# Smaller first loads on two queues, fewer warm-up products and a split that reads the PSUM bank twice, in a two-layer decoder step on one core

## The chip, the core and the metric

The kernel runs on one core of a Trainium2 chip. TensorE (PE) multiplies, VectorE (DVE) and ScalarE (ACT) do elementwise work, GpSimd (POOL) and SyncE (SP) mostly issue DMAs. ACT also issues DMAs from its own queue. The metric is the device time of one execution in microseconds. The time before is the median of three runs.

## The reference, cut to what matters

One inference step of a decoder with two layers, for a prompt of 512 tokens and for 8 samples of one token each, 520 columns in all. Model width 1024, feed-forward width 2816.

```python
for l in range(2):
    x = x + 0.5 * swiglu(rms(x, g[l, 0]), w_gate[l, 0], w_up[l, 0], w_down[l, 0])
    # layer 0: causal pooling over windows 2, 4, 8, 16; layer 1: window attention with sinks
    x = x + mixer(rms(x, g[l, 1]))
    x = x + 0.5 * swiglu(rms(x, g[l, 2]), w_gate[l, 1], w_up[l, 1], w_down[l, 1])
y = rms(x, final_g)
```

`swiglu(h) = (silu(h @ w_gate) * (h @ w_up)) @ w_down`. All inputs are fp32. The study is about the very first part, in which x is loaded and transposed and the first 128 columns of `w_gate[0, 0]` and `w_up[0, 0]` are multiplied with it.

## The kernel before, in words

**Products in three terms.** Each fp32 operand is split into a high part (fp32r) and a rest: ACT writes the high part as a rounded copy (`xh`, `wh`), DVE subtracts it from the source (`xl`, `wl`). A product is the sum of `wh*xh`, `wh*xl` and `wl*xh`. The 520 columns are taken in two halves of 260, so one 128x128 piece of weights costs six PE instructions (function `mm`, L413 to L424).

**Layout.** x stands transposed: eight tiles `x[0..7]` of 128 channels by 520 tokens. Weights arrive in chunks of 1 MB (`raw`, three buffers), are cut into pieces of up to four 128x128 blocks, and each piece is split by ACT (L194, `wh`) and DVE (L195, `wl`). The class `Weights` holds the plan: `chunk` and `piece` enter it, `begin` issues the first loads of a chunk, `load` the rest, `get` returns the next split piece, `prefetch` splits some pieces ahead.

**The start (L662 to L739).** x comes from memory as tokens by channels. Loads `xt` (L667) bring 256 tokens by 256 channels (256 KB) each, so that two loads together hold two tiles; `load_x(nc.sync, ...)` puts them on SP's queue, `load_x(nc.scalar, ...)` on ACT's. `grow` (L671) holds the norm gains, `xs` (L674) the samples. PE multiplies ones with ones (L698, twelve calls, 24 records in the trace, as each fp32 product shows as two) and so is busy until the loads are there. Then it transposes the gains (L699), which ACT copies to `gT` (L700).

`x_tile(k)` (L702 to L718) makes tile k: four transposes of the prompt and one of the samples into a PSUM tile (L707, L709), `xh` by ACT with the gain as scale (L712), a copy of the plain tile to SBUF (by ACT for odd k, L714, by DVE for even k, L716), and `xl` by DVE from that SBUF copy (L717).

**The first products.** Tiles 0 and 1 are made first. Then for each k the six products with the gate piece are issued, tile k+2 is made, and the six products with the up piece follow. So PE does five transposes between the two groups, and the transposes of a tile stand two steps ahead of its products.

**What sets the order.** Instructions passed through `later` keep the program's order; a scheduler orders the others. Each engine runs its own in order, so one that waits holds up all behind it. PSUM has four double banks. In the first phase they are used so: one for the gate accumulator, one that tile 0 has first and the up accumulator after it, one shared in turn by tiles 1, 3, 5, 7, and one by the warm-up and then tiles 2, 4, 6. When two tiles share a bank, the transposes of the later one wait for the last reader of the earlier one. The DMAs on SP's and ACT's queues use eight semaphores in turn: the ninth waits for the first's landing.

After the first phase the squares of x are summed (L366, L368, L370), the row norms are computed (L381 and the lines behind it), and the rest of the first feed-forward follows (L443, L417).

Of the kernel before, what the change touches and what calls it, by code (L numbers as in the profile page):

```python
# [18 lines left out]
P = 128  # L19
# [11 lines left out]
NH = 3  # L31
NPL = (4, 3, 2, 3)
HD = 64
NB = SP // P
# [57 lines left out]
def rows(raw):  # L92

    return raw.rearrange("p k c -> p (k c)").rearrange("p (r k c) -> p r k c", r=2, k=KT)


class Weights:
# [81 lines left out]

    def _split(self, i):  # L180
        nc = self.nc
# [20 lines left out]
    def get(self):  # L202
        self._split(self.ng)
        w = self.items[self.ng][2]
        self.ng += 1
        return w

    def prefetch(self):
        self._split(self.ng - 1 + self.ahead)


@with_exitstack
def yoco_step(ctx, tc, ins, outs):
# [37 lines left out]
    def later(ins):  # L251

        return tc.keep_in_program_order(ins)
# [3 lines left out]

    def ld(dst, src):
        return lambda raw: later(nc.sync.dma_start(dst(raw), src))

# [7 lines left out]
    def plan_ffn(l, f):  # L268
        g3 = w_gate[l, f].rearrange("(k p) c -> p k c", p=P)
        u3 = w_up[l, f].rearrange("(k p) c -> p k c", p=P)  # L270
        d3 = w_down[l, f].rearrange("(k p) c -> p k c", p=P)
        t0 = 0
        for n in PARTS:
            for j in range(t0, t0 + n):
                c = slice(j * P, (j + 1) * P)
                cuts = ((0, 4), (4, 8)) if (l, f, j) == (0, 0, 0) else ((0, 8),)
                ch = W.chunk(
                    *[
                        ld(lambda raw, k=k, o=o: rows(raw)[:, o, k[0] : k[1], :], w3[:, k[0] : k[1], c])
                        for k in cuts  # L280
                        for o, w3 in ((0, g3), (1, u3))
                    ]
                )
                if j < NPL[2 * l + f]:
                    for k0 in (0, 4):
                        for o in (0, 1):
                            W.piece(ch, lambda raw, k0=k0, o=o: rows(raw)[:, o, k0 : k0 + 4, :])
# [372 lines left out]
    with ff_pool() as tmp:  # L660
# [3 lines left out]

        def load_x(eng, c, b2):
            xt[c, b2] = big.tile([P, 2, 256], F32, tag=TT[b2], name="xt")
            later(eng.dma_start(xt[c, b2], xv[:, 2 * b2 : 2 * b2 + 2, c * 256 : (c + 1) * 256]))  # L667

        grow = tmp.tile([48, P], F32, tag="g", name="grow")
        grow2 = tmp.tile([24, P], F32, tag="g", name="grow2")  # L670
        later(nc.scalar.dma_start(grow, norm_g.rearrange("l n (k p) -> (l n k) p", p=P)))  # L671
# [7 lines left out]
        later(S.activation(warm, ones[:, 0:1], AF.Square))  # L679
        for b2 in range(2):  # L680
            load_x(nc.scalar, 1, b2)
        for b2 in range(2):
            load_x(nc.sync, 2, b2)
        W.load(0)
        for b2 in range(2):
            load_x(nc.sync, 3, b2)
        W.load(2)
# [14 lines left out]
        def x_tile(k):  # L702

            pd = duo()
            for b in range(NB):
                src = xt[k // 2, b // 2][:, b % 2, (k % 2) * P : (k % 2 + 1) * P]
                later(T.transpose(pd[:, 0, b * P : (b + 1) * P], src, ident))  # L707
# [4 lines left out]
            later(S.activation(xh, px, AF.Copy, scale=gcol(0, k)))  # L712
            if k % 2:
                later(S.copy(x[k], px))  # L714
            else:
                later(V.tensor_copy(x[k], px))  # L716
            later(V.scalar_tensor_tensor(xl, x[k], gcol(0, k), xh.bitcast(F32), op0=ALU.mult, op1=ALU.subtract))  # L717
            mov0.append((xh, xl))  # L718

        W.pin = later  # L720
        first = duo(), duo()
        x_tile(0)
        ws = [W.get()]
        x_tile(1)
        ws.append(W.get())
        for k in range(KT):
            if k == 3:
                ws = [ws[0], ws[1], W.get(), W.get()]
# [724 lines left out]
```

## Time and profile before

| what | value |
|---|---|
| runs | 1693.46 us median (1693.32 to 1696.6, three runs) |
| profiled execution | 1691.85 us, its span 1690.0 us |
| PE busy | 1657.5 us of the span (98%) |
| mean granted TensorE clock | 0.992 |
| ones, PE L698 | 1.06 to 5.78 us |
| first product, PE L417 | 8.07 us |
| norm's products, PE L381 | from 34.88 us, 1.01 us |

How to read it: the page has busy times by engine and the chain of work that ended last, followed back from the last instruction. The chain in order of time lists pieces with start, length and what. The timeline lists instructions with start, length, engine, line, operation and tiles; `ACTq` and `SPq` are DMA issues; brackets give idle time ahead of the instruction and what ended it. In the table of windows the columns are the stretch, its length, busy time and count for PE, PE's weight loads, DVE, ACT and POOL, then granted clock, DMA share and GB/s.

### The profile page before, as it was taken

Reading aid. Unit: us, or ns where it says so; the run is one execution under the profiler, and the core shown is the slowest. Engines: PE = TensorE matmul, PEld = TensorE weight load, DVE = VectorE, ACT = ScalarE, POOL = GpSimd, SP = SyncE. Lnnn points to the kernel's source line nnn. Section 1 sums busy time; section 2 is a strip of 40 time slices with the busy share of each in tenths; the row PEclk is TensorE's granted clock in tenths of the full one; section 3 lists DMA queues with packets and bytes.
Section 4 is the critical chain, followed back from the end, with each engine's and each line's share of the span. In section 5 each row is a group of like instructions: output and inputs, shape, how many; then the busy total and the mean of one; then the engine's idle time right before and its main releaser. Section 6 shows DMA issues by size and latency. Waiting matters only on the chain.

```text
span 1690.0 us, 34449 instructions
## 1 busy us (share of the span) xinstructions
PE 1657.5 (98%) x13754; PEld 1642.7 (97%) x13754; DVE 1254.4 (74%) x2452; ACT 903.5 (53%) x1793; POOL 142.3 (8%) x176
## 2 busy tenths in 40 slices
PE   9999999999999999999999999999989999999997
PEld 8999999999999999999999999998879999999996
DVE  6866866887875875888775875888876885785776
ACT  6743643665652652656552652655886653463454
POOL 0101101000101101100101101100000100110100
PEclk9999999999999999999999999999899999999998
DMA  8546745652545855634745845642122554674631
GB/s 214 137 128 142 181 134 136 174 167 80 129 140 129 178 147 130 153 117 129 162 137 125 187 137 127 152 138 71 50 51 76 131 137 131 148 173 132 148 109 52
DMA packets 313327, 224.71 MB, mean 133 GB/s; under 512 B 9152, under 2 KB 289320, under 8 KB 313126
## 3 DMA queue, kind: packets, MB, share of 16 engines
q1 hardware_dynamic: 286416, 176.13, 36.8%
q0 software_dynamic: 22432, 40.26, 14.5%
q10 hardware_dynamic: 4318, 6.12, 1.2%
q8 instruction: 108, 1.77, 0.4%
q14 instruction: 53, 0.43, 0.1%
HBM read 180.11 MB, written 5.04 MB: 110 GB/s over the span
## 4 chain that ended last, share of the span: by engine, by line
PE 90%; DVE 4%; ACT 3%; DMA 1%; issue 1%; DVEq 0%; ACTq 0%
PE ps L443 45%; PE ps L417 41%; ACT sm L1121 1%; PE ps L1169 1%; PE ps L814 1%; DVE wl L195 1%; DMA pr<-in_bands_dram 1%; PE ps L839 1%; DVE sm L1101 1%; DVE xl L246 0%; ACT wh L194 0%; PE ps L1146 0%; PE ps L381 0%; PE ps L698 0%; DMA pr<-in_pool_w_dram 0%
## 5 line engine op out<-in xcount | busy, mean ns | idle before, releaser
L194 ACT ACTIVATE wh<-raw 128x512 fp32r<-128x512 f32 (+1 forms) x736 | 446.3, 621 | 544.8 <-PE ps L417 329.5
L195 DVE TENSOR_TENSOR wl<-raw,wh 128x512 fp32r<-128x512 f32 (+1 forms) x736 | 486.9, 676 | 200.7 <-ACT wh L194 197.2
L443 PE MATMUL ps<-th,wh 128*128 128x260 f32 x1216 | 343.7, 283 | 0.0
L443 PE MATMUL ps<-tl,wh 128*128 128x260 f32 x1216 | 343.1, 282 | 0.0
L443 PE MATMUL ps<-th,wl 128*128 128x260 f32 x1216 | 341.5, 282 | 0.0
L417 PE MATMUL ps<-hh,wh 128*128 128x260 f32 x1376 | 284.3, 285 | 2.3 <-DVE mx L1101 1.0
L417 PE MATMUL ps<-hl,wh 128*128 128x260 f32 x1376 | 283.2, 283 | 0.0
L417 PE MATMUL ps<-hh,wl 128*128 128x260 f32 x1376 | 280.7, 282 | 0.0
L443 PEld LDWEIGHTS ps<-tl,wh 128*128 128x128 f32 x1216 | 229.0, 188 | 0.0
L443 PEld LDWEIGHTS ps<-th,wh 128*128 128x128 f32 x1216 | 228.7, 188 | 0.2 <-ACT sa L523 0.2
L443 PEld LDWEIGHTS ps<-th,wl 128*128 128x128 f32 x1216 | 228.1, 188 | 0.0
L417 PEld LDWEIGHTS ps<-hh,wh 128*128 128x128 f32 x1376 | 213.5, 189 | 4.0 <-DVE mx L1101 1.2
L417 PEld LDWEIGHTS ps<-hl,wh 128*128 128x128 f32 x1376 | 215.2, 189 | 0.1
L417 PEld LDWEIGHTS ps<-hh,wl 128*128 128x128 f32 x1376 | 214.0, 189 | 0.0
L443 PE MATMUL ps<-xh,wh 128*128 128x260 f32 x672 | 188.3, 283 | 0.0
L443 PE MATMUL ps<-xl,wh 128*128 128x260 f32 x672 | 188.2, 283 | 0.0
L443 PE MATMUL ps<-xh,wl 128*128 128x260 f32 x672 | 184.2, 282 | 0.0
L159 POOL DMA_DIRECT2D raw<-raw x76 | 65.5, 862 | 1302.8 <-DMA raw<-in_ffn_w_up_dram 438.9
L417 PE MATMUL ps<-xh,wh 128*128 128x260 f32 x736 | 149.4, 285 | 0.6 <-ACT wh L194 0.6
L417 PE MATMUL ps<-xl,wh 128*128 128x260 f32 x736 | 149.5, 284 | 0.5 <-DVE xl L717 0.5
L417 PE MATMUL ps<-xh,wl 128*128 128x260 f32 x736 | 147.8, 283 | 0.1
L591 DVE TENSOR_TENSOR u<-ps,R 128x520 f32<-128x520 f32 (+1 forms) x99 | 67.2, 681 | 106.3 <-PE ps L417 106.3
(260 smaller groups left out, 2849.1 us busy)
## 6 DMA issues: line engine op xcount, KB each, us to landing
raw<-in_ffn_w_gate_dram SPq DMA_DIRECT2D x87, 512.0 KB, 3.9
raw<-in_ffn_w_up_dram SPq DMA_DIRECT2D x87, 512.0 KB, 5.4
raw<-in_ffn_w_down_dram SPq DMA_DIRECT2D x32, 1024.0 KB, 5.3
raw<-raw POOLq DMA_DIRECT2D x76, 256.0 KB, 3.3
S<-in_ffn_w_up_dram SPq DMA_DIRECT2D x76, 256.0 KB, 5.6
S<-raw POOLq DMA_DIRECT2D x76, 256.0 KB, 4.7
raw<-in_ffn_w_down_dram SPq DMA_DIRECT2D x16, 768.0 KB, 4.9
raw<-in_w_q_dram SPq DMA_DIRECT2D x8, 512.0 KB, 4.0
```

Of the source, the lines that this page charges most:

```text
L159: G.dma_start(blk(raw, 2, 1), blk(raw, 1, 1), accum_op=ALU.add)
L194: self.pin(nc.scalar.activation(dh, src, AF.Copy))
L195: self.pin(nc.vector.tensor_tensor(dl, src, dh.bitcast(F32), op=ALU.subtract))
L417: ins = T.matmul(banks[:, hf, :H], a[:, kk, :], hcols(b, hf), start=(first and i == 0), stop=(last and i == 2),)
L443: T.matmul(bank[:, :H], a[:, kk, :], b, start=(not more and kk == 0 and i == 0), stop=(kk == 3 and i == 2), skip_group_check=more,)
L591: V.tensor_tensor(parts(u), bank[:, hfs[0] : hfs[-1] + 1, :H], parts(R[:, c]), op=ALU.mult)
L814: T.matmul(o, a[:, s], b[:, kk, :], start=(n == 0), stop=(n == 5))
L839: T.matmul(po[:, half * 256 : half * 256 + 256], z[:, tau, c], b, start=(i == 0), stop=(i == len(lst) - 1),)
L1101: ins = V.tensor_tensor_reduce(out=sm[:, e * 256 : (e + 1) * 256], in0=self.pe[e][:, bi * 256 : (bi + 1) * 256], in1=cst[:, mk : mk + 256] ...
L1121: S.activation(part(i), part(i), AF.Exp, scale=r8[:, b : b + 1], bias=nm[:, i : i + 1], accum_out=den[:, i : i + 1],)
L1169: T.matmul(po[:, bi * 256 : (bi + 1) * 256], a, p_[:, kc_], start=(n == 0), stop=(n == 3 * len(kts) - 1),)
```

## The change

1. **x in other pieces.** The first 256 channels come as two loads of 512 tokens by 128 channels (256 KB, rows of 512 bytes), one tile each (`load_x1`). All x loads are on SP's queue now.
2. **First weights in smaller pieces.** The first chunk is cut at k = 0 to 2, 2 to 4, 4 to 8 (`FIRST`) instead of 0 to 4, 4 to 8. The gate pieces of the first two cuts are loaded from ACT's queue, everything else from SP's. The six pieces are split one by one; those of two blocks make splits of 128x256.
3. **Order of issue.** SP: x tile 0, up piece 0 to 2, x tile 1, up piece 2 to 4, x for tiles 2 and 3, the pieces 4 to 8, x for tiles 4 to 7, the next chunks. ACT: gains, gate piece 0 to 2, first half of the samples, gate piece 2 to 4, second half of the samples, table load.
4. **Nine calls of ones** (18 records) instead of twelve.
5. **The split reads the bank.** `xl` is computed from the PSUM tile, not from the SBUF copy. The copy to `x[k]` is a function that is called later: after the gate products of step k.
6. `W.prefetch()` at k = 5, 6, 7 becomes `W.ready(W.ng + 3)` at k = 5 and one `prefetch` after the loop; `_split` is called `ready`.

```diff
+FIRST = ((0, 2), (2, 4), (4, 8))
...
+                            nc.scalar if len(cuts) > 1 and o == 0 and k[1] <= 4 else nc.sync,
...
+        load_x1(0)
         later(nc.scalar.dma_start(grow, norm_g.rearrange("l n (k p) -> (l n k) p", p=P)))
-        xs = [big.tile([NS, 512], F32, tag=t, name="xs") for t in HH]
-        for i in range(2):
-            later(nc.scalar.dma_start(xs[i], x_sample[:, 0, i * 512 : (i + 1) * 512]))
-        for b2 in range(2):
-            load_x(nc.sync, 0, b2)
         W.begin(2)
-        warm = cp.tile([P, 1], F32, name="warm")
+        later(nc.scalar.dma_start(xs[0], x_sample[:, 0, :512]))
+        load_x1(1)
+        W.begin(2)
+        later(nc.scalar.dma_start(xs[1], x_sample[:, 0, 512:]))
         later(S.activation(warm, ones[:, 0:1], AF.Square))
...
-        for i in range(12):
+        for i in range(9):
...
             later(S.activation(xh, px, AF.Copy, scale=gcol(0, k)))
-            if k % 2:
-                later(S.copy(x[k], px))
-            else:
-                later(V.tensor_copy(x[k], px))
-            later(V.scalar_tensor_tensor(xl, x[k], gcol(0, k), xh.bitcast(F32), op0=ALU.mult, op1=ALU.subtract))
+            later(V.scalar_tensor_tensor(xl, px, gcol(0, k), xh.bitcast(F32), op0=ALU.mult, op1=ALU.subtract))
             mov0.append((xh, xl))
+
+            def copy():
+                if k % 2:
+                    later(S.copy(x[k], px))
+                else:
+                    later(V.tensor_copy(x[k], px))
+
+            return copy
...
             for o, banks in enumerate(first):
-                mm(ws[k // 4 * 2 + o], k % 4, mov0[k], banks, k == 0, k == KT - 1, pin=later)
-                if not o and k + 2 < KT:
-                    x_tile(k + 2)
-            if k > 4:
-                W.prefetch()
+                w, k0 = ws[k][o]
+                mm(w, k - k0, mov0[k], banks, k == 0, k == KT - 1, pin=later)
+                if not o:
+                    copies.pop(0)()
+                    if k + 2 < KT:
+                        copies.append(x_tile(k + 2))
+            if k == 5:
+                W.ready(W.ng + 3)
+        W.prefetch()
```

In the changed program the engines have this order (a number in brackets is the tile; a letter what it waits for):

```
ACT  gains, gate 0-2, samples 1, gate 2-4, samples 2 (waits for x tile 0's landing), table load, warm,
     gT, wh, constants' load, xh(0), wh, xh(1), xh(2), wh, wh, copy(1), square(0), xa, xh(3), square(1),
     square(2) (waits for DVE's sum), xh(4), wh, wh, copy(3), square(3), xh(5), square(4), xb, xh(6),
     copy(5), square(5), xh(7), 4 wh, copy(7), 2 wh, ...
DVE  wl, xl(0), wl, xl(1), copy(0), xl(2), wl, wl, sum, xl(3), copy(2), sum, sum, xl(4), wl, wl, sum,
     xl(5), copy(4), sum, xl(6), sum, xl(7), 4 wl, copy(6), 2 wl, ...
PE   18 ones, gains, transposes(0), transposes(1), then per k: 6 gate products, transposes(k+2),
     6 up products; the up products of k = 0 wait for copy(0), transposes(k+2) from k = 1 on for copy(k)
```

Much later, in the attention stage of the second layer, the scheduler puts some products, softmax transposes and splits in a different order; the rest of the program keeps its order.

More of the change, by code (lines that the diff above doesn't have):

```diff
@@ L178, in sums, with ready @@
         self.late = (ch, lambda raw: blk(raw, 2, 2))
-    def _split(self, i):
+    def ready(self, i):
         nc = self.nc
@@ L202, in get @@
     def get(self):
-        self._split(self.ng)
+        self.ready(self.ng)
         w = self.items[self.ng][2]
@@ L208, in prefetch @@
     def prefetch(self):
-        self._split(self.ng - 1 + self.ahead)
+        self.ready(self.ng - 1 + self.ahead)
 @with_exitstack
@@ L256, in yoco_step, with ld @@
     W = Weights(nc, rawp, splp, 2, 5)
-    def ld(dst, src):
-        return lambda raw: later(nc.sync.dma_start(dst(raw), src))
+    def ld(dst, src, eng=nc.sync):
+        return lambda raw: later(eng.dma_start(dst(raw), src))
     def plain(ch, kt, col):
@@ L284, in plan_ffn @@
                 if j < NPL[2 * l + f]:
-                    for k0 in (0, 4):
+                    for k0, k1 in cuts if len(cuts) > 1 else ((0, 4), (4, 8)):
                         for o in (0, 1):
-                            W.piece(ch, lambda raw, k0=k0, o=o: rows(raw)[:, o, k0 : k0 + 4, :])
+                            W.piece(ch, lambda raw, k0=k0, k1=k1, o=o: rows(raw)[:, o, k0:k1, :])
                 else:
@@ L705, in x_tile @@
             for b in range(NB):
-                src = xt[k // 2, b // 2][:, b % 2, (k % 2) * P : (k % 2 + 1) * P]
+                if k < 2:
+                    src = xt[0, k][:, b, :]
+                else:
+                    src = xt[k // 2, b // 2][:, b % 2, (k % 2) * P : (k % 2 + 1) * P]
                 later(T.transpose(pd[:, 0, b * P : (b + 1) * P], src, ident))
```

44 lines of the change are left out of this document (29 added, 15 removed).

## The prediction

> **What bounds the kernel now.** I read the page first, then the chain of waits in order of time, then each engine's timeline in the first 25 us.
>
> ```profile
> span 1690.0 us, 34449 instructions
> PE 1657.5 (98%) x13754; PEld 1642.7 (97%) x13754; DVE 1254.4 (74%) x2452; ACT 903.5 (53%) x1793; POOL 142.3 (8%) x176
> PE 90%; DVE 4%; ACT 3%; DMA 1%; issue 1%; DVEq 0%; ACTq 0%
> ```
>
> PE is busy for 98% of the span and carries 90% of the chain, so a microsecond of PE idleness won or added at the start moves the end by as much. The chain there (start, length, what):
>
> ```profile
> 6.81 0.70 ACT xh L712
> ...
> 9.69 0.52 PE ps L417 x2
> 10.20 0.44 PE ps L707 x4
> 10.64 0.15 PE ps L709
> 10.79 1.64 PE ps L417 x12
> 12.43 0.44 PE ps L707 x4
> ...
> 23.39 11.49 PE ps L417 x94
> ```
>
> From 9.69 on the chain is almost PE alone: per tile of x four transposes, a fifth for the samples, twelve products. Only before 9.69 does PE stand idle for long, so only that can be won; what can be lost is that the rest runs without a gap. The timeline, all engines:
>
> ```profile
> 2.18 1.28 ACT L679 ACT_TABLE_LOAD   x1 [2.18 <-issue]
> 2.25 0.48 ACTq L667 DMA_DIRECT2D xt<-in_x_prompt_dram  x1
> ...
> 3.65 1.79 SPq L667 DMA_DIRECT2D xt<-in_x_prompt_dram  x2
> 4.04 0.40 ACTq L667 DMA_DIRECT2D xt<-in_x_prompt_dram  x1
> ...
> 6.00 0.20 ACT L700 COPY gT<-ps 128x48 f32<-128x48 f32 x1 [2.32 <-PE ps L699]
> ...
> 6.81 0.69 ACT L712 ACTIVATE xh<-ps,gT 128x520 fp32r<-128x520 f32 x1 [0.61 <-PE ps L709]
> ...
> 7.40 0.62 ACT L194 ACTIVATE wh<-raw 128x512 fp32r<-128x512 f32 x1
> 7.54 0.70 DVE L716 COPY x<-ps 128x520 f32<-128x520 f32 x1 [6.52 <-ACT xh L712]
> ...
> 7.92 0.69 ACT L712 ACTIVATE xh<-ps,gT 128x520 fp32r<-128x520 f32 x1
> ...
> 8.07 0.50 PE L417 MATMUL ps<-xh,wh 128*128 128x260 f32 x2 [0.63 <-ACT wh L194]
> 8.27 0.76 DVE L717 SCALAR_TENSOR_TENSOR xl<-x,gT,xh 128x520 fp32r<-128x520 f32 x1
> ...
> 8.50 0.59 ACT L714 COPY x<-ps 128x520 f32<-128x520 f32 x1
> 8.95 0.69 DVE L195 TENSOR_TENSOR wl<-raw,wh 128x512 fp32r<-128x512 f32 x1
> ...
> 10.04 0.60 PE L707 MATMUL ps<-ident,xt 128*128 128x128 f32 x4
> 10.15 0.62 ACT L366 ACTIVATE sq<-x 128x520 f32<-128x520 f32 x1
> ...
> 10.68 0.72 ACT L552 ACTIVATE xa<-x,gT 128x520 f32<-128x520 f32 x1
> 10.72 0.51 PE L417 MATMUL ps<-xh,wh 128*128 128x260 f32 x2
> ...
> 11.30 0.67 ACT L712 ACTIVATE xh<-ps,gT 128x520 fp32r<-128x520 f32 x1
> ...
> 12.27 0.60 PE L707 MATMUL ps<-ident,xt 128*128 128x128 f32 x4
> ...
> 14.63 0.60 PE L707 MATMUL ps<-ident,xt 128*128 128x128 f32 x4
> ...
> 21.31 0.60 PE L707 MATMUL ps<-ident,xt 128*128 128x128 f32 x4
> ```
>
> Read from it: a tile's transposes occupy PE for 0.68 (10.04 to 10.72), its twelve products for 1.55 (10.72 to 12.27). ACT and DVE start the next instruction before the last has ended: the next comes 0.59 after xh, 0.52 after wh, 0.53 after a square, 0.62 after xa, 0.68 after xl, so about 0.1 before the end. A dependent on another engine starts 0.03 to 0.06 after the end; I take 0.04.
>
> **The change part by part.** I carry the start of each tile's transposes through, new against old; a tile is numbered 0 to 7.
>
> *The ones.* Six fewer of 24 records end PE's warm-up about 0.7 sooner. It gains nothing: the next instructions wait for x and for ACT, as follows.
>
> *ACT's queue.* The order there is now norm gains, gate piece, samples, gate piece, second half of the samples, table load, warm, gT. The second samples' DMA is the ninth, and waits until the first x piece has landed; behind it stand the table load, warm, gT, and through gT every xh. In the trace before, the load ran at 2.18, hidden. The same wait is visible there on the x load issued at 4.04: it shows 256 KB of x landed by 4.04. SP's pair from 3.65 to 5.44 shows the second 256 KB landed by about 5.04 (the second issue is some 0.4 of it). The new first piece is also 256 KB but shares the engines with gate and gain pieces: between 4.04 and 5.04; I take 4.6. Then an issue of 0.46, the load 1.28, warm and gT 0.2: gT done at 6.55 against 6.20. Next wh of the first gate piece, half as wide: not in the trace, between half of 0.52 and the whole; I take 0.35 (for DVE's half wl likewise, of 0.60). xh(0) from 6.96 to 7.65, first product 7.7 (old 8.07). The constants' load in between is issued by the sequencer, which in the row at 2.25 issued during the table load: 0; if it blocks, 0.48 more.
>
> *The split from the bank.* xl(0) no longer waits for the copy of x: 7.69 to 8.45, product 8.5 (old 9.09), wl is there, and tile 2's transposes could start at 9.1 (old 10.04). xl from the bank is not in the trace; nearest are the copy from the bank, 0.70, and xl from SBUF, 0.76: I take 0.76, between 0.70 and 0.9. Tile 2's second x load follows the smaller pieces; old it had landed by 10.04: between 9.1 and 10.04, I take **9.2**, since no more bytes stand ahead of it than before. So far the change wins 0.84.
>
> *What the split costs.* Tiles' banks are used again: tile k+2's transposes write the bank of tile k (from tile 1 on) and wait for its last reader. That was xh and the copy, early. Now it is the copy, which stands after xl, and further back in its engine's order. Tile 0's bank becomes the accumulator of the up products: they wait for its copy. With the changed program's order on each engine:
> - Copy 0 (DVE): xl(0), wl, xl(1), copy: 8.37+0.35+0.68+0.70 = 10.1. First up product 10.15 (PE ready 9.88). Tile 3 is ready for PE at 10.15+1.55 = 11.7.
> - Copy 1 (ACT): xh(2) at 9.92, two half wh, copy: +0.59+0.35+0.35+0.59 = 11.8. Tile 3 at **11.84** (old 12.27), ends 12.52.
> - Copy 2 (DVE, behind xl(3), which needs xh(3), which stands behind a square and xa): ACT is free of copy 1 at 11.7, +0.53+0.62 = 12.85; xh(3) 0.69, xl(3) 0.68, copy 0.70, handovers: 14.98. PE is ready at 14.07. Tile 4 at **14.98** (old 14.63), ends 15.66.
> - Copy 3 (ACT, behind a square that waits for DVE's sum, xh(4), two whole wh): copy 2 at 14.94, the sum 0.6 later, so the square at 15.58; +0.53+0.59+0.52+0.52+0.59 = 18.33. PE ready 17.21. Tile 5 at **18.37**, ends 19.05.
> - Copy 4 (DVE, as copy 2, without the backlog): 19.09+0.69+0.04+0.68+0.70 = 21.2. PE ready 20.6. Tile 6 at **21.24**, ends 21.92.
> - Copy 5 (ACT, behind a square, xb, xh(6)): 21.24+0.53+0.62+0.59+0.59 = 23.57. PE ready 23.47. Tile 7 at **23.6** (old 21.31): 2.3 late.
> - The next tile's accumulator waits for copy 6, behind xl(7) and four whole wl: xh(7) 24.32 to 25.01, xl 25.05+0.68, 4 x 0.60, copy 0.70: 28.85. PE's thirty products left, 0.12 each (11.49 over 94), and one transpose end at 28.2: 0.65 idle.
>
> ```profile
> 16.88 0.76 DVE L717 SCALAR_TENSOR_TENSOR xl<-x,gT,xh 128x520 fp32r<-128x520 f32 x1
> 17.56 1.29 DVE L195 TENSOR_TENSOR wl<-raw,wh 128x512 fp32r<-128x512 f32 x2
> 18.76 0.69 DVE L370 TENSOR_TENSOR acc<-acc,sq 128x520 f32<-128x520 f32 x1
> ```
>
> (17.56 to 18.76 are two wl: 0.60 each.) Behind that the old order had no gap until 34.88 (23.39+11.49), and I see none in the new one. **Sum: 2.3 + 0.65 = 3.0 us longer.**
>
> *Weights in smaller pieces.* By the chain nothing waits for weights after 9.69; PE's products cover them (the second half is needed only behind tile 5's transposes), and one that came late would cost its delay: 0. *Attention.* The scheduler also puts a few instructions of the attention stage in another order (products, softmax transposes, splits). I cost it at 0, bounds 1.5 us either way: over 1178 to 1262 PE was idle for 12.7 of 84 us.
>
> ```profile
> 1178.00:1262.00 84.00, 71.28 (x554) 63.62 (x552) 67.20 (x263) 69.66 (x201) 0.52 (x1) 0.92 0.15 39
> ```
>
> The profiled execution took 1691.85 us, 1.85 more than its span, and stands 1.6 below the median of 1693.46. Its sum is 1694.9; on the median, **1696.5 us**.
>
> On the banks, the Trainium skill ("PSUM — Partial Sum Buffer", section "PSUM bank collisions raise a hardware error") says that no two engines may touch one bank on the same partitions at once. The trace agrees: DVE's copy at 7.54 starts when xh ends, 7.50. By it xh, xl and the copy go through the bank one after the other, 0.69+0.76+0.70, as I summed; could the copy run beside xl, tiles 4 and 6 would each start some 0.7 sooner and the sum be about 1.6.
>
> **The rivals.**
> 1. *The banks come free in time, the early start is kept.* ACT's and DVE's backlogs (square, xa) would have to fall into PE's waits. For: DVE and ACT are idle for 26% and 47% of the span. Against: even with no backlog the way back, 0.69+0.68+0.70 with handovers 2.15, is longer than PE's 1.55. Then tile 2's 0.84 stays: 1692.6. This decides if tile 4 starts before 14.63.
> 2. *The clock falls.* The granted clock (the third number from the end) falls after a stretch in which PE had little to do:
>
> ```profile
> 373.45:376.86 3.41, 2.30 (x20) 2.10 (x18) 2.73 (x6) 0.91 (x3) 0.00 (x0) 1.00 1.02 284
> 376.86:380.27 3.41, 1.77 (x15) 1.80 (x16) 1.79 (x5) 2.50 (x9) 0.86 (x1) 1.00 0.86 312
> 380.27:383.69 3.42, 3.42 (x19) 3.42 (x18) 2.73 (x13) 1.75 (x5) 0.00 (x0) 0.50 0.59 190
> ```
>
> PE busy for 2.30 of 3.41 kept it, 1.77 lost it for the next 3.41. In my sum the stretch after 4.81 holds the last ones, two tiles' transposes and a first product, about 2.1: in between. Half a clock over 3.41 us loses up to 1.7 us of products, more if it hits twice, or if the shorter warm-up comes too late: 1698.2 to 1700. The Trainium skill ("TensorE: Matmul & The Clock Gate", section "What's actually happening") gives the window as 3413 ns and says that it runs free of the kernel's start; the trace agrees with the length, and by the rule the case would come in some runs only.
> 3. *Attention's new order decides.* Up to 1.5 either way on top of the sum: 1695 to 1698.
>
> **How the numbers follow.** My case, chance 0.62: 1696.5, from 1695.5 (first piece at 4.04: -0.56; xl 0.70 and half splits at half: -0.4) to 1698.5 (piece at 5.04: +0.44; blocked issue +0.48; xl 0.9 in four tiles and half splits at the whole: +1.0). Rival 1: 0.14. Rival 2: 0.14. Rival 3: 0.10. What a measurement of this kernel can tell from no change is about 0.2%, 3.4 us, so the line lies at 1696.9, inside my case: 0.32 of it below, 0.30 above. Faster by more than that: 0.03 of rival 1 and 0.01 of rival 3, 0.04. Same: 0.32+0.11+0.04 = 0.47. Slower: 0.30+0.14+0.05 = 0.49. The range leaves out rival 1 and the worst 0.06 of rival 2: 1692.8 to 1699.6.
>
> **What would show it.** Right: on ACT the table load after 4.5, gT after 6; tile 2's transposes near 9.2; then PE waiting at tiles 4, 5 and 6 for copies of x, tile 7 at 23 to 24, and about 3 us more at the norm's ten products (34.88 old). Wrong: tile 4 at or before 14.6; a granted clock of 0.5 after 8; or a difference that first appears after 1178.

## The result, and the profile after

The changed kernel takes **1700.45 us** (median of six runs, 1699.22 to 1701.6); the kernel before took 1693.54 beside it (1693.3 to 1696.6). The ratio is 1.0037, 95% interval 1.0025 to 1.0049: slower by 7 us, where 3 were forecast and 1699.6 was the end of the range. The profiled execution of the changed kernel took 1701.53 us, span 1699.7. The page of after:

```profile
span 1699.7 us, 34444 instructions
PE 1662.0 (98%) x13748; PEld 1646.6 (97%) x13748; DVE 1254.1 (74%) x2454; ACT 904.0 (53%) x1795; POOL 142.3 (8%) x176
PE 91%; DVE 5%; ACT 3%; issue 1%; DMA 0%; ACTq 0%; DVEq 0%
```

DVE's and ACT's busy times are what they were (1254.4 and 903.5); no work was added. PE is busy for 4.5 us more, on six records fewer, and idle for 5.2 us more (37.7 of the span instead of 32.5). So it worked at a lower clock somewhere, and it also waited. The timeline of after in the start (line numbers are those of the changed kernel: L707 ones, L719 and L721 transposes, L724 xh, L725 xl, L730 and L732 the copies, L422 the products, L386 the norm's):

```profile
4.14 1.28 ACT L689 ACT_TABLE_LOAD   x1 [4.14 <-DMA xt<-in_x_prompt_dram]
5.47 1.12 PE L719 MATMUL ps<-ident,xt 128*128 128x128 f32 x4
5.58 0.20 ACT L709 COPY gT<-ps 128x48 f32<-128x48 f32 x1
5.59 0.35 ACTq L785 DMA_DIRECT2D sel<-in_consts_dram  x1
5.67 0.42 ACT L195 ACTIVATE wh<-raw 128x256 fp32r<-128x256 f32 x1
6.89 0.69 ACT L724 ACTIVATE xh<-ps,gT 128x520 fp32r<-128x520 f32 x1 [0.80 <-PE ps L721]
7.62 0.76 DVE L725 SCALAR_TENSOR_TENSOR xl<-ps,gT,xh 128x520 fp32r<-128x520 f32 x1 [1.07 <-ACT xh L724]
7.64 0.50 PE L422 MATMUL ps<-xh,wh 128*128 128x260 f32 x2
9.02 0.60 PE L719 MATMUL ps<-ident,xt 128*128 128x128 f32 x4
9.30 0.69 DVE L732 COPY x<-ps 128x520 f32<-128x520 f32 x1
10.13 0.48 PE L422 MATMUL ps<-xh,wh 128*128 128x260 f32 x2 [0.36 <-DVE x L732]
11.65 0.66 PE L719 MATMUL ps<-ident,xt 128*128 128x128 f32 x4
14.04 0.69 DVE L732 COPY x<-ps 128x520 f32<-128x520 f32 x1
14.84 0.63 PE L719 MATMUL ps<-ident,xt 128*128 128x128 f32 x4 [0.74 <-issue]
17.54 0.58 ACT L730 COPY x<-ps 128x520 f32<-128x520 f32 x1
18.17 0.66 PE L719 MATMUL ps<-ident,xt 128*128 128x128 f32 x4 [0.93 <-ACT x L730]
20.42 0.69 DVE L732 COPY x<-ps 128x520 f32<-128x520 f32 x1
21.21 0.63 PE L719 MATMUL ps<-ident,xt 128*128 128x128 f32 x4 [0.62 <-issue]
23.58 0.66 PE L719 MATMUL ps<-ident,xt 128*128 128x128 f32 x4
```

The table load waits for x tile 0. Tile 2's transposes come a microsecond earlier than before (9.02 against 10.04). The up products at 10.13 wait for a copy of x, and so do tiles 4, 5 and 6: their brackets show 0.74, 0.93 and 0.62 us of an idle PE. For tile 5 the bracket names ACT's copy; for tiles 4 and 6 it says only `issue`, but DVE's copies end at 14.73 and 21.11, and the transposes start 0.1 us later. The chain of after, pieces in order of time, shows the end of it:

```profile
28.32 0.62 DVE x L732
28.94 0.04 issue
28.98 8.89 PE ps L422 x72
37.88 1.01 PE ps L386 x10
```

The next tile's accumulator waits for the copy of x that ends at 28.94, and the norm's products begin at 37.88, 3.0 us later than the 34.88 of before (in the timeline, which starts an instruction at its weights, 37.72 against 34.72; below I use these). That is the forecast to a tenth. The other 6.7 us of the 9.7 between the two spans lie behind it. The table of windows, from the first to the last product of the scores in the second layer's attention, before and then after:

```profile
1159.68:1269.06 109.38, 96.60 (x775) 87.11 (x776) 89.16 (x354) 84.49 (x245) 0.52 (x1) 0.94 0.21 49
```
```profile
1164.63:1279.06 114.43, 99.12 (x776) 90.03 (x777) 89.07 (x353) 84.71 (x245) 0.52 (x1) 0.91 0.20 47
```

**The attention is 5.05 us longer**, with DVE and ACT busy for the same 89 and 84.5 us, PE for 2.5 more, and a mean granted clock of 0.91 instead of 0.94. From norm to scores the difference is 2.0 (the granted clock stood at 0.5 for 6.83 us at the pool mixer, 382.2 to 389.0, where before it did for 3.41), and behind the attention it is 0.3 the other way: 3.0 + 2.0 + 5.05 - 0.3 = 9.7.

Where the attention waits: some idle times of PE in the same piece of it. Before (L1232 transpose of the sample scores sT, L417 twelve products of the output projection), then after (L1261 and L422):

```profile
1244.32 0.33 PE L1232 MATMUL ps<-ident,sT 128*128 128x128 f32 x1 [0.70 <-DVE sT L1222]
1248.37 0.39 PE L417 MATMUL ps<-hh,wh 128*128 128x260 f32 x1 [0.32 <-ACT pr L1237]
```
```profile
1250.65 0.33 PE L1261 MATMUL ps<-ident,sT 128*128 128x128 f32 x1 [1.45 <-DVE sT L1251]
1255.92 0.52 PE L422 MATMUL ps<-hh,wh 128*128 128x260 f32 x1 [1.65 <-ACT oT L1210]
```

PE waits 0.75 us longer for sT. DVE now splits oT ahead of it, which takes 0.60 (rows of after below, L247 and L1251); in before DVE made sT at 1244.08 and split oT behind it, at 1244.18. The second waits for oT, which ACT now copies behind four exponentials, and the first of those stands waiting for its bias nm (the third row). In before ACT filled that time with the copies of oT, from 1246.37 to 1247.11, and began the exponentials at 1247.14:

```profile
1249.81 0.69 DVE L247 TENSOR_TENSOR hl<-oT,hh 128x512 fp32r<-128x512 f32 x1
1250.41 0.18 DVE L1251 TENSOR_TENSOR sT<-ps,rs 128x32 f32<-128x32 f32 x1
1252.16 0.60 ACT L1150 ACTIVATE sm<-sm,nm,r 128x256 f32<-128x256 f32 x1 [1.51 <-DVE nm L1145]
```

### The profile page after: what moved, and what is told of

Same layout as the page of the kernel before. It is cut to its first block, busy times and chain, and to the rows that moved or that the text cites. A ratio compares the mean times of both kernels' runs of the same rounds, so it can differ in the third digit from the quotient of the medians.

```text
span 1699.7 us, 34444 instructions
## 1 busy us (share of the span) xinstructions
PE 1662.0 (98%) x13748; PEld 1646.6 (97%) x13748; DVE 1254.1 (74%) x2454; ACT 904.0 (53%) x1795; POOL 142.3 (8%) x176
## 3 DMA queue, kind: packets, MB, share of 16 engines
q1 hardware_dynamic: 286960, 176.39, 36.7%
## 4 chain that ended last, share of the span: by engine, by line
PE 91%; DVE 5%; ACT 3%; issue 1%; DMA 0%; ACTq 0%; DVEq 0%
PE ps L448 45%; PE ps L422 41%; ACT sm L1150 1%; DVE wl L196 1%; PE ps L843 1%; PE ps L1198 1%; PE ps L868 1%; DVE sm L1130 1%; DVE xl L247 0%; ACT wh L195 0%; PE ps L386 0%; PE ps L1175 0%; DVE acc L375 0%; PE ps L707 0%; DVE u L596 0%
## 5 line engine op out<-in xcount | busy, mean ns | idle before, releaser
L195 ACT ACTIVATE wh<-raw 128x512 fp32r<-128x512 f32 (+2 forms) x738 | 446.3, 620 | 547.0 <-PE ps L422 330.5
L196 DVE TENSOR_TENSOR wl<-raw,wh 128x512 fp32r<-128x512 f32 (+2 forms) x738 | 486.4, 674 | 208.4 <-ACT wh L195 204.6
L422 PE MATMUL ps<-hh,wh 128*128 128x260 f32 x1376 | 285.6, 286 | 2.7 <-ACT oT L1210 1.6
L422 PE MATMUL ps<-hl,wh 128*128 128x260 f32 x1376 | 284.1, 284 | 0.0
L422 PE MATMUL ps<-hh,wl 128*128 128x260 f32 x1376 | 281.6, 283 | 0.0
L422 PEld LDWEIGHTS ps<-hh,wh 128*128 128x128 f32 x1376 | 214.7, 190 | 4.1 <-ACT oT L1210 1.9
L422 PEld LDWEIGHTS ps<-hl,wh 128*128 128x128 f32 x1376 | 216.1, 190 | 0.3
L422 PEld LDWEIGHTS ps<-hh,wl 128*128 128x128 f32 x1376 | 214.9, 189 | 0.0
L422 PE MATMUL ps<-xh,wh 128*128 128x260 f32 x736 | 149.6, 285 | 1.1 <-DVE x L732 1.0
L422 PE MATMUL ps<-xl,wh 128*128 128x260 f32 x736 | 149.2, 283 | 0.3 <-DVE xl L725 0.3
L422 PE MATMUL ps<-xh,wl 128*128 128x260 f32 x736 | 148.0, 282 | 0.0
```

Source lines behind the costliest of these rows:

```text
L195: self.pin(nc.scalar.activation(dh, src, AF.Copy))
L196: self.pin(nc.vector.tensor_tensor(dl, src, dh.bitcast(F32), op=ALU.subtract))
L422: ins = T.matmul(banks[:, hf, :H], a[:, kk, :], hcols(b, hf), start=(first and i == 0), stop=(last and i == 2),)
```

## The experiments

All kernels were timed in five rounds, each group of them beside runs of the kernel before on the same chip (medians 1693.37, 1693.23, 1693.77, 1693.40 and 1694.41 in the five groups, in the order of the table; single runs from 1690.6 to 1699.8). The ratio is that to the kernel before, with its 95% interval; "norm" is the start of the norm's products in the profiled execution, "attention" the length from the first to the last product of the scores there.

| run | what it is | median us | ratio | norm | attention |
|---|---|---|---|---|---|
| (before) | | see above | 1 | 34.72 | 109.4 |
| (after) | | 1700.45 | 1.0037 [1.0025, 1.0049] | 37.72 | 114.4 |
| order_before | after, attention in before's order | 1695.82 | 1.0004 [0.9993, 1.0014] | 37.73 | 109.7 |
| order_after | before, attention in after's order | 1697.55 | 1.0024 [1.0012, 1.0035] | 36.59 | 114.2 |
| copy_first | order_before without part 5 | 1693.49 | 0.9991 [0.9981, 1.0001] | 36.52 | 109.6 |
| copy_at_once | order_before, copy right behind xl | 1693.09 | 0.9993 [0.9984, 1.0002] | 33.88 | 109.7 |
| oT_late | before, one pair of ACT moved | 1694.71 | 1.0009 [0.9998, 1.0021] | 36.77 | 110.7 |
| oT_early | order_after, that pair moved back | 1697.26 | 1.0024 [1.0011, 1.0037] | 34.30 | 114.2 |
| part5_alone | before with part 5 | 1697.41 | 1.0025 [1.0013, 1.0036] | 39.10 | 108.9 |
| best9 | copy_at_once, table load earlier | 1692.64 | 0.9999 [0.999, 1.0008] | 33.50 | 109.5 |
| dve_after | before, DVE alone in after's order | 1700.4 | 1.0043 [1.003, 1.0056] | 34.36 | 116.8 |
| act_pe_after | before, ACT and PE in after's order | 1701.64 | 1.0037 [1.0024, 1.0051] | 38.49 | 114.4 |
| best6 | best9, other ones | 1692.76 | 0.9994 [0.9986, 1.0003] | 34.94 | 109.4 |
| ones12 | order_before with twelve ones | 1696.23 | 1.001 [1.0001, 1.0019] | 37.98 | 111.1 |
| fill_before | before with fillers | 1694.61 | 1.0006 [0.9995, 1.0016] | 34.74 | 110.8 |
| fill_after | after with fillers | 1698.21 | 1.003 [1.0018, 1.0043] | 37.78 | 112.9 |
| fill_best | best9 with fillers | 1692.3 | 0.9981 [0.9969, 0.9993] | 33.52 | 111.8 |
| fill2_before | before, one filler fewer | 1693.89 | 1.0004 [0.9994, 1.0014] | 38.40 | 112.1 |
| fill2_after | after, one filler fewer, one more | 1702.01 | 1.0044 [1.003, 1.0058] | 37.75 | 113.9 |
| fill2_best | best9, one filler fewer | 1692.53 | 0.9988 [0.9979, 0.9998] | 33.78 | 109.7 |

**Order against start: order_before and order_after.** The scheduler's order of the attention is written down as a table of the instructions' places, and each instruction is tied behind its neighbour by an edge that orders issue and makes nobody wait:

```diff
+ORDER = {"PE": (...), "DVE": (...), "Activation": (...)}
...
+    for name, runs in ORDER.items():
+        own = [i for i in traced if str(i.engine).split(".")[-1] == name][::-1]
+        chain = [own[r] for a, b in runs for r in range(a, b - 1, -1)]
+        for p, q in zip(chain, chain[1:]):
+            tc.add_manual_dep(q, p.name, info, reason="order")
```

> The changed kernel whole, but PE, DVE and ACT issue the second layer's attention in the order that the kernel before has there (pinned by edges that set the order of issue and wait for nothing). Theory A (the start costs 3.0, the attention's new order the rest of the 7.0): the attention's share goes, 1693.5 + 3.0 = 1696.5 us, and the stretch from 1250 to 1275 adds less than 1 us; no half clock behind 1250. Theory B (the order is innocent: arriving 3 us later puts the attention at another point of the clock's windows, and those do it): 1700, and half-clock windows behind 1250 stay.

> The kernel before whole, start included, but PE, DVE and ACT issue the second layer's attention in the order that the changed kernel has there. Theory A (the order costs what the start doesn't): 1693.5 + 4.0 = 1697.5 us, norm's products at 34.9 as before, the difference appears between 1250 and 1275 together with a granted clock of 0.5 there. Theory B (windows alone): 1693.5.

Measured 1695.82 and 1697.55, within 0.7 and 0.1 us of theory A. (The norm's products of order_after start at 36.59, not at 34.9: in its profile the granted clock was 0.5 from 11.25 to 14.66.) The windows of the attention, order_before and then order_after:

```profile
1164.46:1274.17 109.71, 96.68 (x775) 87.20 (x776) 89.28 (x355) 84.56 (x245) 0.52 (x1) 0.94 0.22 49
```
```profile
1162.83:1277.05 114.22, 101.40 (x776) 92.12 (x776) 89.26 (x354) 84.61 (x245) 0.52 (x1) 0.88 0.21 47
```

The length goes with the order, not with the time at which the attention is reached: order_before comes there at the changed kernel's time and needs 109.7, order_after earlier and needs 114.2. Theory B is out. By the medians about 4.2 of the 7 us are the order's and 2.4 the start's. The order's part is clear of noise (1.0024, interval 1.0012 to 1.0035). The start's is not in this run, whose interval, 0.9993 to 1.0014, holds no change; part5_alone below shows it clear of noise.

**The start: copy_first, copy_at_once, part5_alone.** All three have before's order in the attention. copy_first:

```diff
-            later(V.scalar_tensor_tensor(xl, px, gcol(0, k), xh.bitcast(F32), op0=ALU.mult, op1=ALU.subtract))
+            if k % 2:
+                later(S.copy(x[k], px))
+            else:
+                later(V.tensor_copy(x[k], px))
+            later(V.scalar_tensor_tensor(xl, x[k], gcol(0, k), xh.bitcast(F32), op0=ALU.mult, op1=ALU.subtract))
```

In copy_at_once the first line stays and the four lines of the copy stand behind it. In both the function that copies later is gone. part5_alone is the kernel before with part 5 of the change's diff and nothing else.

> The changed kernel without its part 5: the copy of x directly behind xh, xl from that copy, as in the kernel before; the attention pinned in the order of before. Theory A (the deferred copies hold the banks, and that is the whole loss of the start): no waits for copies, xl(0) at 8.4 to 9.15, tile 2's transposes at 9.7 (10.04 before, 9.02 after), norm's products at 34.5 and 1693.5 - 0.35 = 1693.1 us. Rival C (the smaller pieces, the two queues and the late table load cost the start its time too): tile 2 later than 10.04 or gaps for weights behind it, norm's products behind 35, over 1694.

> The changed kernel with xl still read from the bank, but the copy of x issued directly behind xl instead of behind the gate products of its step; the attention pinned in the order of before. Theory A (it is the place of the copy in its engine's order, not the second read of the bank): a tile's bank is free 2.2 us behind its transposes, PE comes back to it only 3.8 us behind them, so no wait; tile 2 at 9.0, then every 2.23 us, norm's products at 34.88 - 0.9 = 34.0 and 1692.6 us. Rival D (the bank read twice in row is too slow in itself): waits for copies stay at tiles 4 to 7, norm's products at 36 or later, 1695 or more.

> The kernel before (its loads, its four weight pieces, its twelve ones) with part 5 alone: xl from the bank, the copies of x deferred to behind the gate products; the attention pinned in the order of before. Theory A (the deferred copies are the start's whole loss): first product at 8.1 as before, PE waits for copies from tile 4 on, tile 7 at 23.5 to 24 (21.31 before), norm's products at 37.5 to 38.2, 1693.4 + 3.0 = 1696.4 us. Rival C (the smaller pieces and the moved table load have a share in it): norm's products before 36.5, under 1695.

copy_at_once: norm at 33.88 as theory A said (34.0), where order_before, which differs from it by the place of the copy alone, has 37.73, and no wait for a copy. The median is 1693.09 beside 1695.82; the two intervals overlap. Its timeline, DVE's xl and copy of tile 0 and the transposes of tiles 2, 3 and 4:

```profile
7.41 0.76 DVE L796 SCALAR_TENSOR_TENSOR xl<-ps,gT,xh 128x520 fp32r<-128x520 f32 x1 [0.82 <-ACT xh L795]
8.09 0.69 DVE L800 COPY x<-ps 128x520 f32<-128x520 f32 x1
8.81 0.60 PE L790 MATMUL ps<-ident,xt 128*128 128x128 f32 x4
11.02 0.60 PE L790 MATMUL ps<-ident,xt 128*128 128x128 f32 x4
13.27 0.60 PE L790 MATMUL ps<-ident,xt 128*128 128x128 f32 x4
```

Tiles follow each other by 2.2 us, PE's own pace; tile 4 is at 13.27 where the changed kernel had it at 14.84. Rival D is out: the second read of the bank costs nothing here, the place of the copy did. part5_alone shows the same from the other side (PE of part5_alone, L778 the transposes of tiles 4, 5 and 6):

```profile
15.99 0.63 PE L778 MATMUL ps<-ident,xt 128*128 128x128 f32 x4 [0.63 <-issue]
19.08 0.66 PE L778 MATMUL ps<-ident,xt 128*128 128x128 f32 x4 [0.67 <-ACT x L789]
22.12 0.63 PE L778 MATMUL ps<-ident,xt 128*128 128x128 f32 x4 [0.60 <-issue]
```

Norm at 39.10 and 1697.41 us, both about 1 us more than forecast. Its first product comes at 8.63, where 8.1 was expected. From the first product to the norm's it takes 30.5 us, after 30.1 and before 26.7: part 5 makes the loss, with the old loads as with the new. copy_first is no clean test: PE waits for no copy there to free a bank, but in its profile the clock stood at 0.5 from 8.3 to 15.2, which hides what the start would have been. Its 36.52 is on rival C's side, its median of 1693.49 on theory A's, and it says no change within 0.2%.

**Which part of the order: oT_late, oT_early, dve_after, act_pe_after.** Only the table of places is edited.

> The kernel before whole, with its own order of the attention pinned, save one pair: ScalarE's two copies of oT that empty one unit's values bank (in the profile before at 1246.37, ahead of the four exponentials from 1247.14) are issued behind those exponentials, as the changed kernel does. Theory A1 (this pair makes the order's loss: the twelve products of the output projection behind it take that bank and wait): PE waits some 1.5 to 2.5 us for oT ahead of the twelve products, the clock falls there in addition, 1695.5 to 1697 us. Rival A2 (the loss comes from the other moves, VectorE's scaling of the softmax ahead of the sample scores above all): under 0.7 more, 1693.4 to 1694.1.

> The kernel before with the attention in the changed kernel's order, save the same pair: the two copies of oT stand ahead of the exponentials, as before. Theory A1: most of the 4.2 us of the run order_after goes, 1693.8 to 1695. Rival A2: it stays, 1697 us or more.

> The kernel before whole; in the attention PE and ScalarE keep the order of the kernel before, VectorE alone takes the changed kernel's order (softmax scaling ahead of the next scores' reductions, the sample scores sT behind the split of oT, the chain for the next exponentials' bias nm later). Theory A3 (VectorE's order makes the loss: PE waits 1.4 us for sT instead of 0.7, and again for what hangs on nm): 1693.3 + 3 = 1696 to 1697.5 us, sT's wait at 1.4. Rival A4 (ScalarE's and PE's orders make it): 1693.3 to 1694.

> The reverse: in the attention PE and ScalarE have the changed kernel's order, VectorE that of the kernel before. Theory A3: no more than the oT pair gave, 1693.5 to 1695 us. Rival A4: 1696.5 to 1697.5.

The pair alone costs 1.3 us of attention (110.7), and putting it back into the new order gives nothing (114.2): A1 fell. Then A3 and A4 both fell, with times above either forecast (1700.4 and 1701.64): DVE's order alone and ACT's with PE's alone each cost as much as both together or more. Windows of dve_after, then act_pe_after:

```profile
1159.55:1276.37 116.82, 103.85 (x776) 94.20 (x777) 88.84 (x353) 84.81 (x245) 0.52 (x1) 0.87 0.20 46
```
```profile
1165.04:1279.44 114.40, 99.47 (x775) 89.61 (x776) 88.53 (x353) 84.73 (x245) 0.52 (x1) 0.91 0.20 47
```

No single instruction was found that carries the loss. What is shown is that the orders of the engines belong together: one engine's new order beside the others' old ones costs as much as all of it, with the same work done.

**Clock or waits: the runs with fillers.** In the attention PE is idle for 12.6 to 13.2 us in most of these runs, whichever order (15 in after and act_pe_after); what grows is the time at half clock (13.65 us before, 20 to 31 with the new order). So the loss could be the half clock that PE's waits set off. Products of ones were put where PE waits for data:

```diff
+    def fill(out, *site):
+        for i in range(FILL.get(site, 0)):
+            FILLS.append(T.matmul(out, ones, ones, start=True, stop=True).ins)
...
+                    fill(po[:, bi * 256 : bi * 256 + P], "values", self.t, self.h, bi)
```

> The kernel before with its own order everywhere, and products of ones (their results are overwritten by the next product, which starts afresh) where PE waits for data: eleven calls ahead of the norm's products at the pool mixer (wait 2.75 us), ten and nine ahead of the first two groups of the first values (2.48 and 2.03), three ahead of the sample scores' transpose (0.70). A call is 0.23 us, so they end about when the wait does. Theory A5 (PE's waits cost by the half clock that follows them): no 0.5 at 380 and at 1182 to 1193, where 3.4 and 10.2 us stood with PE busy for 3.4 and 7.9 of them at half speed: 1693.4 - (3.4 + 7.9)/2 = 1687.8, with what the fillers overrun 1688 to 1690 us. Rival A6 (products at half clock lie beside ScalarE's and VectorE's chain, which sets the attention's time; the half clock hides): 1692.5 to 1693.5.

> The changed kernel whole, its attention's order pinned as it is, with the same fillers, six calls ahead of the sample scores' transpose (its wait is 1.45 there). A5: the same 4 to 5 us and one of the two windows that the new order adds: 1700.4 - 4.5 - 1.5 = 1694.5, 1693.5 to 1696 us. A6: 1699 or more.

> best9 (1692.6) with the fillers of fill_before, the attention in the order of before. A5: 1692.6 - 4.5 = 1688 us, under both kernels. A6: 1692 to 1692.6.

The ten calls ahead of the first values were a mistake: they needed the bank that the products behind them waited for, started only at 1182.30, ran at half clock from 1182.86, and took 4.1 us on the path (PE of fill_before, L493 the fillers):

```profile
1182.30 4.13 PE L493 MATMUL ps<-ones 128*128 128x128 f32 x20 [2.38 <-DVE mx L1225]
1186.12 0.55 PE L1294 MATMUL ps<-xh,tl 128*128 128x256 f32 x2
```

> As fill_before without the ten calls ahead of the first values: those waited for the same bank as the products behind them, ran at half clock from 1182.3 and held the products up by 4.1 us. Eleven calls ahead of the norm's products at the pool mixer, nine ahead of the first values' second group, three ahead of the sample scores' transpose stay. A5 (the half clock costs): 0.5 for one window at 1182 instead of three, none or one at the mixer, 1693.4 - 1.2 - 2 = 1690.2 us, 1689.5 to 1691.5. A6 (it hides): 1693 or more.

> The changed kernel with its own order pinned and the same fillers, six calls ahead of the sample scores' transpose and six more into the wait for oT (1.64 us) ahead of the twelve products of the output projection, into the half of a bank that is written next; the waits of order stay as they are. A5 (the new order costs by the half clock it sets off): no half clock from 1250 to 1262, the distance to fill2_before falls from 7.0 to about the start's 3.0 plus 0.5 to 1.5, 1694 to 1695 us. A6 (the order's waits cost by themselves): the distance stays at 6.5 to 7, 1697 us.

> best9 with the fillers of fill2_before and the order of before in the attention. A5: best9 (1692.6) less 3 us, 1689.5, between 1688.5 and 1690.5 us, under both kernels by 0.2%. A6: 1692.

Without them the kernel before gained nothing (1693.89 beside 1694.41), and fill2_after became no faster than after, though from 1249.5 to the last scores its clock was never granted less than full:

```profile
1249.54:1276.41 26.87, 22.56 (x197) 20.53 (x198) 15.97 (x72) 17.95 (x58) 0.00 (x0) 1.00 0.19 40
```

Its attention still took 113.9. By total time A6 has the better of it: fill_best and fill2_before lie where A6 put them, fill2_best 0.5 and fill_before 1.1 us above, fill_after (1698.21) between the two forecasts, and fill2_after (1702.01) above both, 8.1 us from fill2_before. But the totals hide two parts. Split the attention at the first of the twelve products of the output projection (lengths in us; "half" is the time in them at a granted clock of 0.5):

| profile | order | first scores to these products | half | these products to last scores | half |
|---|---|---|---|---|---|
| before | before | 88.69 | 13.65 | 20.69 | 0 |
| ones12 | before | 88.81 | 13.65 | 22.23 | 3.4 |
| fill2_before | before | 88.28 | 13.7 | 23.78 | 6.8 |
| after | after | 91.29 | 13.65 | 23.14 | 6.8 |
| fill_after | after | 90.67 | 13.65 | 22.26 | 3.4 |
| fill2_after | after | 93.70 | 17.1 | 20.23 | 0 |

Behind the products the length goes with the half clock, whichever order: in the twenty profiles 20.2 to 20.7 with none (eight of them), 21.9 to 22.3 with one window (six), 23.0 to 25.0 with two (five), 27.9 with three (dve_after). It doesn't hide there: in the chain of after these twelve products take 2.90 us, in that of fill2_after, with the same order, 1.45. Ahead of the products after needs 2.6 us more than before with the same time at half clock, and the chain has that time on ACT (36.1 us instead of 34.3) and DVE (36.7 instead of 36.0), not on PE. **Of the 5.05 us of after, about 2.6 are the order's waits and 2.45 half clock behind them.**

So A6 is right ahead of the products and A5 behind them, and fill2_after's total hides it: its filler ahead of the output projection itself waited 3.10 us for a bank and began those products 2.4 us later than in after (93.70 against 91.29), which took back most of what the clock gave (20.23 against 23.14). Two things stay open: that the longer waits set off the half clock is likely, but no run shows it step by step; and the other profiles with the new order divide otherwise (order_after has 7.1 us more of half clock than before ahead of the products too).

**ones12, best9, best6.**

> The changed kernel with twelve calls of ones as before, the attention pinned in the order of before (as in order_before, 1695.8). Theory A (the ones are a cover and cost nothing while x and ScalarE are late; PE would end them at 6.0, xh(0) would start at 6.8 as with nine): 1695.8, norm's products at 37.9. Rival F (nine ones are too few for the clock, twelve hold it up through the first transposes): 1695.2 or less. Third way: they are on the path now, and gT comes 0.7 later: 1696.4.

> As copy_at_once, and ScalarE's table load stands ahead of the second samples' DMA, so that it waits for no landing; the attention in the order of before. Theory A (the load behind the landing of x tile 0 delays gT and through it everything up to the first product): the load at about 3.0, gT at 5.5 (then limited by the ones), first product at 6.8 instead of 7.4 to 7.7, tile 2 at 8.4, norm's products 0.5 earlier than in copy_at_once, 1692.5 us. Rival E (the next landing takes its place, x tile 1 or 2 or a weight piece): first product or tile 2 where copy_at_once has them, 1693.1.

> As best9 (xl from the bank, the copy directly behind it, the table load ahead of the second samples), with six calls of ones instead of nine, and five calls of ones between the transposes of tile 0 and of tile 1, where PE otherwise waits for x tile 1; the attention in the order of before. Theory A (in best9 the ones still set gT, at 5.5): gT at 4.5, xh(0) at 5.1, first product at 6.8 behind tile 1's transposes (x tile 1 lands at 6.4), then tile 2 where its second load lands, at 8.9: nothing more than best9, 1692.6 us. Rival E2 (the start is a sum of PE times, every product brought ahead counts): 1692.2.

ones12: with twelve calls the ones end at 6.05, gT comes at 6.29 instead of 5.58 and the first product at 7.84 instead of 7.64: 0.25 at the norm (37.98 against 37.73). That is the third way: twelve calls are on the path. The removal gained no more than this, and the medians of 1696.23 and 1695.82, 2.46 and 2.45 above the kernel before of their groups, show no difference. best9 moves one line:

```diff
-        later(nc.scalar.dma_start(xs[1], x_sample[:, 0, 512:]))
         later(S.activation(warm, ones[:, 0:1], AF.Square))
+        later(nc.scalar.dma_start(xs[1], x_sample[:, 0, 512:]))
```

Its ACT, and its first product:

```profile
2.89 1.28 ACT L759 ACT_TABLE_LOAD   x1 [2.89 <-issue]
5.49 0.20 ACT L780 COPY gT<-ps 128x48 f32<-128x48 f32 x1 [1.10 <-PE ps L779]
7.19 0.51 PE L493 MATMUL ps<-xh,wh 128*128 128x260 f32 x2
```

The load waits for nothing, gT now waits for the ones, and the norm's products start at 33.50, the earliest of all. The first product comes at 7.19, not at the 6.8 expected, and the time can't be told from copy_at_once (0.9999 and 0.9993). In best6 the clock came up at 10.15 only, its fillers ran at half speed and held up tile 1: 34.94. fill_best and fill2_best are the two versions whose interval lies below the kernel before, by 0.19% and 0.12%; their medians are 0.1 to 0.3 us from best9's, whose own interval holds no change. So two versions measured faster than the kernel before, by one or two tenths of a percent; among eighteen versions that is little.

## Why the prediction was wrong, step by step

- **The ones** (six records fewer gain nothing): right within the 0.25 us of ones12.
- **ACT's queue**: the wait was there, the sizes were off and made up for each other. x tile 0 landed by 3.82, not at 4.6, so gT was done at 5.78, not 6.55. But tile 0's four transposes of the prompt took 1.12 (tile 2's took 0.60): the trace's record of a full clock begins only at 6.75. xh waited for them until 6.89 (6.96 forecast). That the first product came at 7.64 (7.7) was luck. The constants' load beside wh (5.59 and 5.67) cost nothing, as taken.
- **The split from the bank**: 0.76, as taken; tile 2 at 9.02 (9.2). On the banks, the Trainium skill ("PSUM — Partial Sum Buffer", section "PSUM bank collisions raise a hardware error") says that two engines may not access one bank on the same partitions at the same time. This trace and copy_at_once agree: the copy follows xl, never beside it (tile 1 of copy_at_once: DVE's xl ends at 9.78, ACT's copy starts at 9.97).
- **The stalls**: the up products 10.13 (10.15 forecast), tile 3 at 11.65 (11.84), tile 4 at 14.84 (14.98), tile 5 at 18.17 (18.37), tile 6 at 21.21 (21.24), tile 7 at 23.58 (23.6), the accumulator at 28.98 (28.85), norm 3.0 later (3.0). This part of the chain was right in mechanism and size.
- **Weights in smaller pieces, 0**: right; no product waits for weights behind 9.02.
- **The step that failed: "*Attention.* ... I cost it at 0, bounds 1.5 us either way".** It costs 5.0 us in the profiled execution and 4.2 in the medians of order_after. The argument was PE's idle time there (12.7 of 84 us), as if that bounded what an order can cost. But in this stretch the chain that ended last goes round three engines, each of which keeps its order (in before it runs through DVE for 38 us of the 109, ACT for 34 and PE for 33). With the same busy times of DVE and ACT the stage grew by 5 us when the order changed: in after by 2.6 us of waits and by 2.45 us at half clock behind them. Rival 3 named the new order, with the same bound and a chance of 0.10.
- **From the profiled execution to the median (+1.6)**: this probably stood for half clock that is missing with the changed start. The start of the kernel before was profiled eight times (before, order_after, oT_late, oT_early, dve_after, act_pe_after, fill_before, fill2_before): four times the norm's products start at 34.3 to 34.7, twice at 36.6 to 36.8, twice at 38.4 to 38.5, mean 36.05; in the later four the granted clock is 0.5 for one or two windows behind the first products. The changed start was profiled four times (after, order_before, fill_after, fill2_after): 37.7 to 37.8 each, with no half clock there. Against the start that the prediction was worked out from, the change loses 3.0; on the mean 1.7. order_before measures 2.4 in its median and 0.04% (0.7 us) in its ratio.
- **Rival 2, the clock falls**: at the start it does so in four of the eight profiles of the kernel before's start, and in none of the four of the changed one. The windows of fill2_before, whose start is that of before:

```profile
6.99:10.41 3.42, 2.29 (x14) 1.55 (x13) 1.89 (x3) 2.71 (x6) 0.00 (x0) 1.00 1.08 327
10.41:13.82 3.41, 3.31 (x15) 2.83 (x14) 2.35 (x5) 2.52 (x5) 0.00 (x0) 0.50 1.07 305
```

  The first full window begins at 4.81 in before, at 4.42 in order_after and at 6.99 here. By the Trainium skill ("TensorE: Matmul & The Clock Gate", section "What's actually happening") the window runs free of the kernel's start; these traces agree.
- **Rival 1** didn't happen: tile 4 is later than 14.63.

## What to carry to other kernels

When an instruction is deferred that is the last reader of a shared buffer, follow it in its own engine's order to the next writer: here the copy cost 3.9 us at the norm's products by its place (37.73 against 33.88), and its reading of the bank made PE wait nowhere. Where a scheduler sets the order, a change anywhere can alter the order somewhere else; compare the orders, and cost such a difference by the chain of the stage it falls in, not by PE's idle time, and count in the half clock that new waits can bring. One profiled execution is one draw: where the clock can fall, take the start from several.

## What the runs showed that was not expected

The share of a window in which PE is busy doesn't alone decide on the next window's clock. 2.29 of 3.42 us lost it in the rows above, where 2.30 kept it in the prediction's rows, and 1.56 lost it in before, at 1233.61; in fill2_after 1.55 kept it (rows of before, then of fill2_after; the third number from the end is the granted clock):

```profile
1233.61:1237.02 3.41, 1.56 (x13) 1.27 (x11) 2.58 (x15) 3.28 (x11) 0.00 (x0) 1.00 0.46 135
1237.02:1240.43 3.41, 3.05 (x14) 2.83 (x16) 2.68 (x11) 2.53 (x8) 0.00 (x0) 0.50 0.88 175
```
```profile
1252.95:1256.37 3.42, 1.55 (x13) 1.55 (x14) 1.69 (x6) 2.73 (x9) 0.00 (x0) 1.00 0.00 0
1256.37:1259.78 3.41, 3.41 (x31) 3.23 (x29) 0.36 (x2) 1.64 (x6) 0.00 (x0) 1.00 0.00 0
```

And the kernel's scatter has causes that a trace shows: one or two windows of half clock behind the first products, some 2 us each at the norm's products, and one or two at the pool mixer.
